# Expert pairs of a routed block: three groups of one-hot sums, and a first weight group of four planes

## The chip, the cores and the metric

The kernel runs on one core of a Trainium2 chip. The metric is the device time of one execution in microseconds (us); lower is better. Everything is float32 at the interface. Engines are named as in the profile: PE (TensorE matmul), PEld (its weight loads), DVE (VectorE), ACT (ScalarE), POOL (GpSimd), SP (SyncE, whose queue issues nearly all DMAs).

## The reference, cut to what matters

The program is a whole block (recurrent branch, sparse attention, routed experts) followed by two layers of a second block. The change touches only the routed experts: 512 tokens, each sent to 2 of 32 experts, each expert a gated pair of products.

```python
def expert_block(args):
    xb, e = args
    hid = jax.nn.silu(xb @ w1[e]) * (xb @ w3[e])     # w1, w3: 1024 x 512
    return hid @ w2[e]                               # w2: 512 x 1024
ys = lax.map(expert_block, (xs, blk_exp)).reshape(n_rows, D_)
out = jax.ops.segment_sum(ys * row_gate[:, None], row_tok, num_segments=T)
...
h = h + g2[:, None, :] * hier_moe(u2, ...)
```

Each expert has three matrices of 2 MiB (2.1 MB), 201 MB in all, and each is read once.

## The kernel before

**The stage.** The experts are worked in 16 pairs (loop at L1452). Each expert has 64 slots, so a pair fills 128 rows: `pair_gather` (L1354) fetches their tokens, `pair_tokens` (L1357) turns them on PE (tile `xgt`) into `xx`. `pair_in` (L1373) makes the two products with W1 and W3 (PE tile `e`, weights `w`), `hidden` (L1269) the gated value on ACT and DVE, `pair_out` (L1400) turns it (`hdt`) and makes the product with W2 (weights `w2r`). These matmuls are float32. `both` (L1368) issues one for each expert of the pair: expert 0 on columns 0 to 63 of the array, expert 1 on columns 64 to 127; each stands in the trace as two instructions. A pair has 64 such instructions on `w` and 32 on `w2r`.

**The one-hot sums.** `outputs` (L1282) scales the result into `y`, splits it into `yh` and `yl` (ACT, then DVE), and returns the generator `combine` (L1295). Each of its 8 steps is one PSUM bank: two matmuls (L1301 with `yl`, L1302 with `yh`) on the whole array, and a DVE add into `h` (L1303). The generator is handed to the `pair_in` after next as `beside`, and in the source one step stands after each of its 8 groups of planes (L1386). PSUM banks for `cmb`, `xgt` and `hdt` come from one tag of three buffers (`tr`).

**Weight buffers.** The 8 planes of W1, and those of W3, are read in four groups of 2 planes, 512 KB per expert and group, in rows of 4 KB, into buffers of the tags PG, PG, WH, WL (L1381). The tag PG has 24 buffers (four are held through this stage: two token pages, `g2R` and a page of small tables), WH and WL have 3 each. W2 is read by `pair_loads` (L1390) as 8 loads of 512 KB into PG. So a pair has 24 loads of 512 KB: 16 PG and 4 each of WH and WL. The tag RAW (3 buffers of 8 KB per partition, 1 MB each) isn't used by the pairs. It serves the dense products before (`TM` and `FM`, L342 and L393) and after.

**The branch.** Ahead of the pairs stands `more(CAP)` (L1449, body L1424 to L1441): a branch that runs only where an expert has more than 64 tokens. Its body, with `expert_in` (L1318) and `expert_out` (L1333), uses RAW, WH and WL. A buffer of a tag that the body uses can't be filled for the pairs ahead of the branch.

**Order.** An engine runs its instructions in one fixed order, but this is not the order of the source: the tile framework chooses it when the program is built, by dependences and its own forecast of when each is ready. The order that came out is read in the trace.

Of the kernel before, what the change touches and what calls it, by code (L numbers as in the profile page):

```python
# [10 lines left out]
F32 = mybir.dt.float32  # L11
F32R = mybir.dt.float32r
# [52 lines left out]
def build(ctx, tc, I, out, dbg=None):  # L65
# [6 lines left out]
    load = nc.sync.dma_start  # L72
# [3 lines left out]
    def t_(shape, dt, tag, name):  # L76
        uid[0] += 1
        return sb.tile(shape, dt, tag=tag, bufs=NB[tag], name=f"{name}_{uid[0]}")

    def pg(name, dt=F32R, shape=(128, 2, 512)):  # L80
        return t_(list(shape), dt, "PG", name)

    def pt_(name, dt=F32R, shape=(128, 2, 512)):
        return t_(list(shape), dt, "PT", name)
# [31 lines left out]
    def sg(name, w=512, dt=F32):  # L116
        return t_([128, w], dt, "SG", name)

    def sa(name, w=512, dt=F32):
        return t_([128, w], dt, "SA", name)  # L120
# [4 lines left out]
    def mmp(name, tag="mm"):  # L125
        uid[0] += 1
        return pp.tile([128, 512], F32, tag=tag, bufs=dict(mm=4, tr=3, po=1)[tag], name=f"{name}_{uid[0]}")

    def trp(name):
        return mmp(name, "tr")  # L130
# [4 lines left out]
    def f(ap):  # L135
        return ap.bitcast(F32)

    def split(hi, lo, src, eng=None):
        S.copy(hi, src)  # L139
        (eng or V).tensor_tensor(lo, src, f(hi), OP.subtract)  # L140
# [144 lines left out]
    def mm3(ps, l, r, start, stop):  # L285

        mmk(ps, [(l, r)], start, stop)

    def mmk(ps, pairs, start, stop):

        for n, (l, r) in enumerate(pairs):
            PE.matmul(ps, l[0], r[1], start=start and n == 0, stop=False)  # L292
            PE.matmul(ps, l[1], r[0], start=False, stop=False)  # L293
        for n, (l, r) in enumerate(pairs):
            PE.matmul(ps, l[0], r[0], start=False, stop=stop and n == len(pairs) - 1)  # L295
# [287 lines left out]
    ps = fm.tile(4352, 72)  # L583
# [6 lines left out]
    ps = trp("wit")  # L590
# [371 lines left out]
    for d in range(8):  # L962
        ps = fmb.tile(128 * d)
# [7 lines left out]
        p = pg("mT")  # L971
        hi, lo = (p[:, n].rearrange("p (c r) -> p r c", r=8) for n in range(2))
# [112 lines left out]
    ps = trp("lgt")  # L1085
# [37 lines left out]
    ps = trp("rank")  # L1123
# [92 lines left out]
    def normalizer(gvec, bvec, dst, paged=True):  # L1216

        gR = row("lng", gvec, True)
        bR = row("lnb", bvec, True)
        pages = []  # L1220

        def norm(i, v, mv, var, later=None):
            r = rsqrt(var, 1, lambda: V.scalar_tensor_tensor(v, v, mv[:, 0:1], gR, OP.subtract, OP.mult))
            for cs in (slice(0, 512), slice(512, 1024)):
                V.scalar_tensor_tensor(v[:, cs], v[:, cs], r, bR[:, cs], OP.mult, OP.add)
                if not paged:
                    load(dst(i)[:, :, cs], v[:, cs])
            if not paged:
                return
            if later is None:  # L1230
                turn(i, v)
            else:
                later.append(lambda: turn(i, v))

        def turn(i, v):
            if not pages:
                pages.extend(pg("xT") for _ in range(8))
            tk = slice(i * 128, (i + 1) * 128)
            for q in range(2):
                b = trp("xt")  # L1240
                for k in range(4):
                    PE.transpose(b[:, k * 128:(k + 1) * 128], v[:, (4 * q + k) * 128:(4 * q + k + 1) * 128], ident)
                for k in range(4):
                    kk, c = 4 * q + k, slice(k * 128, k * 128 + 128)
                    split(pages[kk][:, 0, tk], pages[kk][:, 1, tk], b[:, c])
            load(dst(i), v)

        return norm, pages
# [6 lines left out]
    def rows_of(t):  # L1255
        return lambda i: t[i * 128:(i + 1) * 128, :]
# [12 lines left out]
    def hidden(p1, p3):  # L1269
        hd = sg("hid")  # L1270
        S.activation(hd, p1, AF.Tanh, scale=0.5)
        V.scalar_tensor_tensor(hd, hd, 1.0, p1, OP.add, OP.mult)
        V.scalar_tensor_tensor(hd, hd, 0.5, p3, OP.mult, OP.mult)
        return hd
# [43 lines left out]
    def expert_in(W1, W3, xh, xl):  # L1318
        pss = []
        for W in (W1, W3):  # L1320
            ps = mmp("e1")
            for q in range(4):
                raw = t_([128, 2, 512], F32, "RAW", "w13")
                load(raw, W[q * 256:(q + 1) * 256, :].rearrange("(k p) n -> p k n", p=128))
                hi = t_([128, 2, 512], F32R, "WH", "wh")
                lo = t_([128, 2, 512], F32R, "WL", "wl")
                split(hi, lo, raw)
                mmk(ps, [((xh[:, 2 * q + k], xl[:, 2 * q + k]), (hi[:, k], lo[:, k])) for k in range(2)],
                    q == 0, q == 3)
            pss.append(ps)  # L1330
        return hidden(*pss)

    def expert_out(hd, W2):  # L1333
        b = trp("hdt")
        for k in range(4):
            PE.transpose(b[:, k * 128:(k + 1) * 128], hd[:, k * 128:(k + 1) * 128], ident)
        hp = pt_("hp")
        split(hp[:, 0], hp[:, 1], b)
        py = [mmp("e2") for _ in range(2)]
        for k in range(4):  # L1340
            raw = t_([128, 1024], F32, "RAW", "w2r")
            load(raw, W2[k * 128:(k + 1) * 128, :])
            hi = t_([128, 1024], F32R, "WH", "wh")
            lo = t_([128, 1024], F32R, "WL", "wl")
            split(hi, lo, raw)
            for m in range(2):
                cs = slice(m * 512, m * 512 + 512)
                ks = slice(k * 128, k * 128 + 128)
                mm3(py[m], (hp[:, 0, ks], hp[:, 1, ks]), (hi[:, cs], lo[:, cs]), k == 0, k == 3)
        return py  # L1350


# [15 lines left out]
    def both(ps, lhs, rhs, start, stop):  # L1368
        for h in range(2):
            hs = slice(CAP * h, CAP * h + CAP)  # L1370
            PE.matmul(ps[hs], lhs[:, hs], rhs[h], start=start, stop=stop)  # L1371

    def pair_in(j, xT, beside):  # L1373
        pss = []
        for nm in ("moe_w1", "moe_w3"):
            W = [I[nm][0, 2 * j + h].rearrange("(p a) n -> p a n", a=8) for h in range(2)]
            ps = mmp("e1")
            for q in range(4):
                ws = []
                for h in range(2):  # L1380
                    raw = t_([128, 2, 512], F32, ("PG", "PG", "WH", "WL")[q], "w13")  # L1381
                    load(raw, W[h][:, 2 * q:2 * q + 2])
                    ws.append(raw)
                for k in range(2):
                    both(ps, xT[:, 2 * q + k], [w[:, k] for w in ws], q + k == 0, q + k == 4)
                next(beside, None)  # L1386
            pss.append(ps)
        return hidden(*pss)

    def pair_loads(j):  # L1390
        W = [I["moe_w2"][0, 2 * j + h].rearrange("(p a) n -> p a n", a=4) for h in range(2)]
        ws = []
        for k in range(4):
            for h in range(2):
                raw = pg("w2r", F32, (128, 1024))
                load(raw, W[h][:, k])
                ws.append(raw)
        return ws

    def pair_out(j, hd, ws):  # L1400
        b = trp("hdt")
        cols = hd.rearrange("p (a j) -> p j a", j=4)
        for k in range(4):
            PE.transpose(b[:, k * 128:(k + 1) * 128], cols[:, k], ident)
        hp = sg("hp")
        S.copy(hp, b)
        py = [mmp("e2") for _ in range(2)]
        for k in range(4):
            for m in range(2):
                cs = slice(m * 512, m * 512 + 512)  # L1410
                both(py[m], hp[:, k * 128:k * 128 + 128], [w[:, cs] for w in ws[2 * k:2 * k + 2]], k == 0, k == 3)
        return outputs(py, gt0[:, j:j + 1], rows0[:, :, j])
# [33 lines left out]
    beside = iter(())  # L1446
# [5 lines left out]
    for j in range(17):  # L1452
# [7 lines left out]
        if j == 16:  # L1460
            fgR = row("fgR", I["final_g"])
            norm, xT = normalizer(I["ln_in_g_2"], I["ln_in_b_2"], rows_of(xres[0]))
            nav_tm = nav_weights(0).prepare()
        if prev is not None:
            for _ in beside:
                pass
            beside = pair_out(j - 1, prev, pair_loads(j - 1))
# [477 lines left out]
    xT, nav_tm = layer(0, xT, nav_tm, xres[0], xres[1], rows_of(xres[2]))  # L1945
# [32 lines left out]
```

## Time and profile before

| | us |
|---|---|
| median of 3 runs | 3155.69 (3153.24 to 3157.79) |
| the profiled execution | 3154.16 |
| its span, first to last instruction | 3152.4 |
| PE busy in the span | 2970.1 (94%) |
| DVE, ACT, POOL busy | 1848.6, 1131.5, 279.6 |
| expert stage, from the first expert matmul to the last | 664.5 to 1206 |
| TensorE clock granted, mean | 0.984 |

The span was recorded in one execution of 3154.16 us, 1.5 us under the median. All rows below are of that execution. Times in rows are us from the span's start unless marked ns; a row's "idle before" names what ended the idle time. "PEclk" is the granted share of TensorE's full clock, "DMA" the mean busy share of the core's 16 DMA engines.

### The profile page before, as it was taken

How to read it: one execution, taken by the hardware profiler on the slowest of the kernel's cores; microseconds unless marked ns; L12 is line 12 of the kernel's file. 1: busy time of each engine (PE TensorE's matmuls, PEld its weight loads, DVE VectorE, ACT ScalarE, POOL GpSimd, SP SyncE). 2: the span in 40 equal slices, each digit the busy share in tenths (PEclk: the TensorE clock that was granted, in tenths of full speed). 3: DMA queues.
4: the chain of work that ended last, by engine and by line, in shares of the span. 5: the costliest groups of instructions: out<-in, count | busy, mean ns of one | idle time of the engine just before them, and what ended most of it. 6: DMA issues, size and time to landing. Idle time of an engine off the chain costs nothing.

```text
span 3152.4 us, 36476 instructions
## 1 busy us (share of the span) xinstructions
PE 2970.1 (94%) x13749; PEld 2204.3 (70%) x13749; DVE 1848.6 (59%) x3521; ACT 1131.5 (36%) x1986; POOL 279.6 (9%) x263
## 2 busy tenths in 40 slices
PE   6988999979999998999999999999999999999998
PEld 5766777733333335878867788888888876788887
DVE  6899888633223227555589754434545588764434
ACT  4555244210000003444567332222444576432221
POOL 2133000300000000221000200000221000200000
PEclk9989999989999999999999999999999999999999
DMA  6222756679999995432233623243433234632341
GB/s 222 92 90 65 233 185 195 208 289 353 362 372 377 358 376 193 137 114 94 76 112 111 231 100 107 92 142 100 147 117 101 79 99 116 225 107 93 107 139 62
DMA packets 296257, 534.17 MB, mean 169 GB/s; under 512 B 30279, under 2 KB 172789, under 8 KB 296071
## 3 DMA queue, kind: packets, MB, share of 16 engines
q1 hardware_dynamic: 293480, 527.46, 48.5%
q0 software_dynamic: 2304, 4.20, 0.5%
q8 instruction: 110, 1.80, 0.2%
q14 instruction: 77, 0.62, 0.1%
q10 hardware_dynamic: 286, 0.09, 0.0%
HBM read 486.50 MB, written 44.38 MB: 168 GB/s over the span
## 4 chain that ended last, share of the span: by engine, by line
PE 64%; DVE 7%; issue 3%; DMA 2%; ACT 2%; POOL 1%; SPq 0%; DVEq 0%; POOLq 0%; ACTq 0%
PE e L1371 12%; PE fm L292 9%; PE fm L295 9%; PE fm L293 9%; PE ffo L295 2%; PE ffo L293 2%; PE ffo L292 2%; PE cmb L1301 1%; PE cmb L1302 1%; POOL tl L1634 1%; DVE xT L140 1%; DMA w2r<-in_moe_w_dram 1%; PE mix L292 1%; PE mix L295 1%; PE mix L293 1%
## 5 line engine op out<-in xcount | busy, mean ns | idle before, releaser
L140 DVE TENSOR_TENSOR wl<-raw,wh 128x1024 fp32r<-128x1024 f32 (+3 forms) x403 | 462.3, 1149 | 313.8 <-ACT wh L139 312.2
L139 ACT CAST wh<-raw 128x1024 fp32r<-128x1024 f32 (+3 forms) x403 | 388.6, 966 | 543.0 <-PE fm L295 224.2
L292 PE MATMUL fm<-xT,wh 128*128 128x512 f32 (+1 forms) x1264 | 481.9, 384 | 0.0
L293 PE MATMUL fm<-xT,wl 128*128 128x512 f32 (+1 forms) x1264 | 479.9, 382 | 1.3 <-DVE wl L140 1.3
L295 PE MATMUL fm<-xT,wh 128*128 128x512 f32 (+1 forms) x1264 | 301.9, 381 | 0.0
L1371 PE MATMUL e<-w,xx 128*64 128x512 f32 x1024 | 293.8, 605 | 0.0
L293 PEld LDWEIGHTS fm<-xT,wl 128*128 128x128 f32 x1264 | 238.2, 188 | 46.7 <-DVE wl L140 1.7
L292 PEld LDWEIGHTS fm<-xT,wh 128*128 128x128 f32 x1264 | 238.2, 189 | 45.1
L295 PEld LDWEIGHTS fm<-xT,wh 128*128 128x128 f32 x1264 | 231.6, 188 | 45.5
L1371 PEld LDWEIGHTS e<-w,xx 128*64 128x64 f32 x1024 | 79.2, 137 | 138.6 <-issue 130.0
L293 PE MATMUL fm<-uT,wl 128*128 128x512 f32 (+1 forms) x360 | 145.3, 403 | 3.8 <-DVE wl L140 3.8
L1303 DVE TENSOR_TENSOR h<-h,cmb 128x512 f32<-128x512 f32 x128 | 84.6, 686 | 109.2 <-PE cmb L1302 108.5
L1371 PE MATMUL e<-w2r,hp 128*64 128x512 f32 x512 | 141.9, 607 | 3.6 <-DMA w2r<-in_moe_w_dram 2.1
L292 PE MATMUL fm<-uT,wh 128*128 128x512 f32 (+1 forms) x360 | 145.0, 404 | 0.0
L292 PE MATMUL ffo<-wl,hid 128*128 128x512 f32 x352 | 137.1, 390 | 0.0
L293 PE MATMUL ffo<-wh,hid 128*128 128x512 f32 x352 | 136.9, 389 | 0.0
L1371 PEld LDWEIGHTS e<-w2r,hp 128*64 128x64 f32 x512 | 52.8, 137 | 87.9 <-issue 64.5
L1921 DVE SCALAR_TENSOR_TENSOR ffs<-ffs,fm 128x512 f32<-128x512 f32 x44 | 30.3, 688 | 137.7 <-ACT ffs L1920 137.7
L295 PE MATMUL ffo<-wh,hid 128*128 128x512 f32 x352 | 108.4, 389 | 0.0
L139 ACT CAST yh<-y 128x512 fp32r<-128x512 f32 x32 | 19.8, 618 | 224.2 <-DVE y L1292 224.2
L1923 DVE SCALAR_TENSOR_TENSOR ffs<-ffs,fm 128x512 f32<-128x512 f32 x44 | 30.3, 688 | 114.4 <-PE fm L295 114.4
L1634 POOL TENSOR_TENSOR tl<-ml,tl 128x512 f32<-128x512 f32 x32 | 47.7, 1497 | 554.3 <-DVE tl L1630 540.6
(603 smaller groups left out, 5955.6 us busy)
## 6 DMA issues: line engine op xcount, KB each, us to landing
w<-in_moe_w_dram SPq DMA_DIRECT2D x256, 512.0 KB
raw<-in_w_in_dram SPq DMA_DIRECT2D x71, 1024.0 KB
w2r<-in_moe_w_dram SPq DMA_DIRECT2D x128, 512.0 KB
raw<-in_w_ffn_in_dram SPq DMA_DIRECT2D x44, 1024.0 KB
raw<-in_w_mod_dram SPq DMA_DIRECT2D x42, 512.0 KB
raw<-in_w_ffn_out_dram SPq DMA_DIRECT2D x20, 1024.0 KB
raw<-in_w_out_dram SPq DMA_DIRECT2D x12, 1024.0 KB
t_d<-bg SPq DMA_DIRECT2D x48, 256.0 KB
```

The costliest lines, as they stand in the source:

```text
L139: S.copy(hi, src)
L140: (eng or V).tensor_tensor(lo, src, f(hi), OP.subtract)
L292: PE.matmul(ps, l[0], r[1], start=start and n == 0, stop=False)
L293: PE.matmul(ps, l[1], r[0], start=False, stop=False)
L295: PE.matmul(ps, l[0], r[0], start=False, stop=stop and n == len(pairs) - 1)
L1301: PE.matmul(ps, pl, yl[:, cs], start=True, stop=False)
L1302: PE.matmul(ps, pl, yh[:, cs], start=False, stop=True)
L1303: V.tensor_tensor(h1[i][m], h1[i][m], ps, OP.add)
L1371: PE.matmul(ps[hs], lhs[:, hs], rhs[h], start=start, stop=stop)
L1634: G.tensor_tensor(th, m, th, OP.add)
L1921: V.scalar_tensor_tensor(s, s, 1.0, pgt, OP.add, OP.mult)
L1923: V.scalar_tensor_tensor(s, s, 0.5, pup, OP.mult, OP.mult)
```

## The change

Three edits, all in the routed experts.

1. `pair_in`: W1 is read in groups of 4, 2 and 2 planes (tags RAW, PG, PG), W3 in four groups of 2 (PG, PG, WH, WL). The group of 4 planes is 1 MB per expert in rows of 8 KB. A pair then has 22 loads: 2 RAW of 1 MB, 16 PG, 2 WH and 2 WL of 512 KB.
2. `pair_in`: the steps of `combine` stand in the source in three groups: 3 after the second group of W1, 3 after the first group of W3, 2 after the third of W3.
3. `expert_in` and `expert_out`, in the branch's body only: the raw weights go to buffers of 512 columns of the tags SG and SA instead of RAW.

```diff
@@ expert_in @@
             for q in range(4):
-                raw = t_([128, 2, 512], F32, "RAW", "w13")
-                load(raw, W[q * 256:(q + 1) * 256, :].rearrange("(k p) n -> p k n", p=128))
                 hi = t_([128, 2, 512], F32R, "WH", "wh")
                 lo = t_([128, 2, 512], F32R, "WL", "wl")
-                split(hi, lo, raw)
+                for k in range(2):
+                    raw = sg("w13")
+                    load(raw, W[(2 * q + k) * 128:(2 * q + k + 1) * 128, :])
+                    split(hi[:, k], lo[:, k], raw)
@@ expert_out @@
         for k in range(4):
-            raw = t_([128, 1024], F32, "RAW", "w2r")
-            load(raw, W2[k * 128:(k + 1) * 128, :])
...
             for m in range(2):
...
+                raw = sa("w2r")
+                load(raw, W2[ks, m * 512:m * 512 + 512])
+                split(hi[:, m], lo[:, m], raw)
+                mm3(py[m], (hp[:, 0, ks], hp[:, 1, ks]), (hi[:, m], lo[:, m]), k == 0, k == 3)
@@ pair_in @@
-        for nm in ("moe_w1", "moe_w3"):
+        for n, nm in enumerate(("moe_w1", "moe_w3")):
             W = [I[nm][0, 2 * j + h].rearrange("(p a) n -> p a n", a=8) for h in range(2)]
             ps = mmp("e1")
-            for q in range(4):
+            k = 0
+            for tag, w, banks in ((("RAW", 4, 0), ("PG", 2, 3), ("PG", 2, 0)), (("PG", 2, 3), ("PG", 2, 0), ("WH", 2, 2), ("WL", 2, 0)))[n]:
                 ws = []
                 for h in range(2):
-                    raw = t_([128, 2, 512], F32, ("PG", "PG", "WH", "WL")[q], "w13")
-                    load(raw, W[h][:, 2 * q:2 * q + 2])
+                    raw = t_([128, w, 512], F32, tag, "w13")
+                    load(raw, W[h][:, k:k + w])
                     ws.append(raw)
-                for k in range(2):
-                    both(ps, xT[:, 2 * q + k], [w[:, k] for w in ws], q + k == 0, q + k == 4)
-                next(beside, None)
+                for m in range(w):
+                    both(ps, xT[:, k + m], [r[:, m] for r in ws], k + m == 0, k + m == 7)
+                k += w
+                for _ in range(banks):
+                    next(beside, None)
             pss.append(ps)
```

## Rows read from the trace of the kernel before

**Rows 1.** The page's 40 equal slices: PE and DMA, busy tenths.
```profile
PE   6988999979999998999999999999999999999998
DMA  6222756679999995432233623243433234632341
```

**Rows 2.** Windows: stretch, then busy us (count) by engine, PEclk, DMA share, GB/s.
```profile
645.00:650.00 5.00, 0.01 (x1) 0.01 (x1) 4.74 (x27) 0.43 (x3) 0.00 (x0) 0.68 0.00 0
...
655.00:660.00 5.00, 1.91 (x9) 1.77 (x9) 1.97 (x13) 0.00 (x0) 1.95 (x2) 0.50 0.22 49
...
662.70:1196.00 533.30, 514.70 (x1938) 193.70 (x1938) 165.57 (x246) 48.95 (x81) 14.07 (x14) 1.00 0.96 367
...
770.79:1152.19 381.40, 370.45 (x1366) 138.06 (x1364) 116.20 (x173) 32.62 (x56) 8.93 (x9) 1.00 0.96 369
```

**Rows 3.** The same view: one pair, a stretch at full DMA share, and a later dense stage.
```profile
910.71:945.07 34.36, 33.35 (x126) 12.47 (x124) 10.79 (x16) 2.97 (x6) 0.99 (x1) 1.00 0.95 369
...
1150.00:1200.00 50.00, 45.24 (x157) 16.59 (x156) 20.74 (x29) 6.96 (x10) 0.00 (x0) 0.97 1.00 383
...
2000.00:2060.00 60.00, 60.00 (x267) 49.67 (x266) 26.41 (x34) 14.17 (x18) 0.00 (x0) 1.00 0.32 105
```

**Rows 4.** Chain that ended last, pair 1 and pair 2: start us, us, engine, tile, line, count.
```profile
720.67 1.87 PE e L1371 x8
722.54 0.43 PE cmb L1301
722.97 0.23 PE cmb L1302
...
735.12 0.74 DVE y L1292
```

**Rows 5.** The same chain in one later pair, and its first row of the last whole period.
```profile
913.40 1.86 PE e L1371 x6
915.26 0.43 PE cmb L1302
915.69 0.24 PE cmb L1301
915.92 0.23 PE cmb L1302
916.15 1.00 PE e L1371 x2
...
929.62 15.43 PE e L1371 x64
...
1152.19 0.75 DVE y L1292
```

**Rows 6.** Timeline of PE: start, us, line, operation, tile, shape, count [idle before <- releaser].
```profile
662.66 1.94 PE L1364 MATMUL xgt<-ident,xg 128*128 128x128 f32 x8 [5.76 <-DVEq L1424]
...
912.12 0.50 PE L1301 MATMUL cmb<-yl,place 128*128 128x512 f32 x1 [0.96 <-DVE yl L140]
...
1187.26 0.50 PE L1301 MATMUL cmb<-yl,place 128*128 128x512 f32 x1 [1.44 <-DVE yl L140]
...
1191.67 0.40 PE L1302 MATMUL cmb<-yh,place 128*128 128x512 f32 x1
```

**Rows 7.** What the SP queue waited for, 735 to 1152 us: total, times, longest.
```profile
SPq L1382 <- PE e L1371: 132.2, 24, 8.7
SPq L1382 <- DMA w2r<-in_moe_w_dram: 94.0, 96, 1.6
```

**Rows 8.** Timeline of SP around the branch: DMA issues in order, with counts.
```profile
588.61 21.55 SPq L1382 DMA_DIRECT2D w<-in_moe_w_dram  x11
...
637.69 0.44 SPq L1396 DMA_DIRECT2D w2r<-in_moe_w_dram  x1
662.73 2.85 SPq L1382 DMA_DIRECT2D w<-in_moe_w_dram  x6
```

**Rows 9.** Groups by line, 735.12 to 1152.19 us: busy, mean ns | idle before, releasers.
```profile
L1303 DVE TENSOR_TENSOR h<-h,cmb 128x512 f32<-128x512 f32 x96 | 63.9, 686 | 90.6 <-PE cmb L1302 90.1
```

More of the change, by code (lines that the diff above doesn't have):

```diff
@@ L1340, in expert_out @@
         for k in range(4):
-            raw = t_([128, 1024], F32, "RAW", "w2r")
-            load(raw, W2[k * 128:(k + 1) * 128, :])
-            hi = t_([128, 1024], F32R, "WH", "wh")
-            lo = t_([128, 1024], F32R, "WL", "wl")
-            split(hi, lo, raw)
+            ks = slice(k * 128, k * 128 + 128)
+            hi = t_([128, 2, 512], F32R, "WH", "wh")
+            lo = t_([128, 2, 512], F32R, "WL", "wl")
             for m in range(2):
-                cs = slice(m * 512, m * 512 + 512)
-                ks = slice(k * 128, k * 128 + 128)
-                mm3(py[m], (hp[:, 0, ks], hp[:, 1, ks]), (hi[:, cs], lo[:, cs]), k == 0, k == 3)
+                raw = sa("w2r")
+                load(raw, W2[ks, m * 512:m * 512 + 512])
+                split(hi[:, m], lo[:, m], raw)
+                mm3(py[m], (hp[:, 0, ks], hp[:, 1, ks]), (hi[:, m], lo[:, m]), k == 0, k == 3)
         return py
```

## The prediction

> **What bounds the kernel now.** I read the slices of the page first, to see where the change can act [rows 1]: from about 660 to 1206 us, and nowhere else, PE and DMA are both at 9 tenths. So two limits lie close together, and the question is which one holds the other. The windows give the size [rows 2]: from 662.70 to 1196.00 the stage moves 533.3 us x 367 GB/s = 195.7 MB at a DMA share of 0.96, while PE is busy 514.70 of 533.30. In the eleven periods from 770.79 to 1152.19 a pair takes 381.40 / 11 = 34.67 us, and moves 34.67 x 369 = 12.8 MB.
>
> Three views tell the limits apart. In one pair PE is idle 1.0 of 34.36 us [rows 3], and nearly all of that is one wait of 0.96 us for `yl` [rows 6]: weights are there when PE wants them. The SP queue, on the other side, spent 132.2 us of twelve periods waiting for PE to free a weight buffer, 24 times [rows 7]: two a period, as many as W3's loads that find WH and WL still full. It waited for earlier DMAs as well (94.0 us in one row), so the reserve is small: the share of 0.96 becomes 1.00 where PE does not hold the loads back, and the rate there is 383 GB/s [rows 3]. I read: PE's order is the bound, transport stands 4% behind it.
>
> Where PE's 34.67 us go is in the chain. In pair 1, eight matmuls of `e` in one run take 1.87 us, and one bank of sums 0.43 + 0.23 [rows 4]; this is the order of the source. From pair 2 on the order is another: 2 matmuls, three of the sums, 6 matmuls, three of the sums [rows 5]. Two on their own take 1.00 and six take 1.86, so these eight need 2.86 instead of 1.87. The two are those of expert 0 alone; the other half of the array stands empty for them, and expert 1's are missing their partner later. The split lies where expert 0's load is there and expert 1's isn't yet, in the forecast that ordered them. Four groups of a pair (all of W1) are split so, until no sums and turns are left to put in; after that 64 run in 15.43 us [rows 5], 0.24 each. In pair 1 a group with its bank took 1.87 + 0.43 + 0.23 = 2.53 us, less than a split group alone. The first of the twelve periods starts at 735.12 [rows 4] and the last ends at 1152.19 [rows 5].
>
> **The change part by part.** *Split groups.* Each costs 2.86 - 1.87 = 0.99 us, four a pair: 3.96 of the 34.67 [rows 4, 5]. The first group is now two loads of 1 MB. The gap between expert 0's and expert 1's data there is twice as long, so it takes twice as many of the 28 instructions that are put in (16 sums, 12 turns), and the remaining fourteen matmuls of the group run whole. I take two split groups instead of four: -1.98 a pair. Ends: one left (-2.97), or all four (0).
>
> *Runs of sums.* The sums of a pair stand in six runs now; the first matmul of a run takes 0.43 against 0.23 or 0.24 of the next [rows 5]. Three runs instead of six save 3 x 0.20 = 0.60; ends 0 and -0.80. The Trainium skill, page "TensorEngine Tiling (Array Packing)", section "Tiling Modes", says that changing the tiling mode drains TensorE. By that rule alone, fewer switches would be the whole of this edit: 12 x 0.60 = 7 us. The trace agrees that a switch costs, but shows 0.20 us for it, and 0.99 for a split group beside it.
>
> *What grouping adds.* If the sums come straight behind the W2 product, PE waits for the whole chain `y`, `yh`, `yl`: 1.44 us, as at 1187.26, instead of 0.96 [rows 6]: +0.48, ends 0 and +0.48. Queued behind that wait is all of `e`, PE being in order. And a bank must be added into `h` before the fourth next one has a buffer: DVE needs 686 ns a bank [rows 9], PE 0.47. Eight banks in a row took from 1187.26 to 1192.07 [rows 6], 4.81 us against 16 x 0.234 = 3.74. In runs of three or four banks I take a third of that difference, +0.36; ends 0 and +1.07. DVE has the room: 63.9 us of adds in 417.
>
> PE's period: 34.67 - 1.98 - 0.60 + 0.48 + 0.36 = 32.9 us; ends 30.9 and 36.2.
>
> *Buffers.* W1 and W3 used four WH and four WL loads a pair with three buffers each; now it is two and two, and two of RAW with three buffers. The two SP waits a period for W3's buffers should go, since the next use of a WH buffer is a pair later. What is late next is transport itself: 12.8 MB at 383 GB/s is 33.4 us. This lies above PE's 32.9, so the bound passes to the DMAs.
>
> *Ahead of the branch.* SP issued 20 loads of experts from 588.61 to 637.69, as many as PG has free buffers, and then six at once at 662.73, three WH and three WL, behind the branch [rows 8]. In between the DMAs stood still: share 0.00 at 645 to 650 [rows 2]. With RAW out of the branch's body three loads of 1 MB can go ahead of it: 3.15 MB less to move behind 662.7. SP must wait for the dense product of the mix to release RAW, and the stores of `u_d` stand behind it; the idle stretch covers several us of that, and without this cover the delay would reach the token gather. I put it at 0.
>
> *Rows of 8 KB.* A sixth of the bytes. No row shows such a load. The nearest are the full rate of 383 with 4 KB rows and, with 1 KB rows, 105 GB/s at a share of 0.32, or 328 [rows 3]: 17% in two doublings. One doubling for a sixth of the bytes is at most 1.4%, 7 us, in either direction. I take 0, the value of the nearest row.
>
> *The branch's body.* No instruction of L1425 to L1441 ran, so its new loads cost nothing. PE waits 5.76 us behind the branch [rows 6]; a body of another length could move that by a us, up or down; I take 0. If a count passed 64 the body would run, and 8 loads of W2 in place of 4 would show.
>
> *The sum.* 195.7 - 3.15 = 192.6 MB. At full share, 383 GB/s, that is 502.8 us, 30.5 less than 533.3. At today's 367 it is 524.7, 8.6 less. I take a share of 0.98 (375 GB/s), halfway between the two rows, because limits of 32.9 and 33.4 us still delay each other: 513.5 us, 19.8 less. What comes behind 1196 (the last W2 product and its sums) is unchanged. 3154.2 - 19.8 = 3134 us, made against the profiled execution, which lies 1.5 us under the median.
>
> **The rivals.** *Transport is full already.* Share 0.96 may be all there is with gaps between loads, and the 132 us of SP waits only order what would wait anyway. For it: SP's waits for DMAs are as long together. Against it: 383 at share 1.00. It gives 0 to 8.6 us, the lead alone: 3150. The Trainium skill, page "DMA: Bandwidth & Descriptors", section "Bandwidth", names about 358 GB/s as what HBM gives one core; by that rule no order of PE could bring anything. The 367 over 533 us is already above it, so the trace does not agree with it as a ceiling.
>
> *It does not do what it says.* The order comes from the build's forecast, not from the source: today "eight single banks" are six runs. All four groups may stay split. Then PE gains 0.60 and pays 0 to 0.84 a pair: 3151, give or take 6. For it: the pattern of rows 5 has stood in twelve pairs alike.
>
> *Slower.* The sums land as one block ahead of `e`, and the splits stay. The place is the head of each pair: PE waits 0.48 longer and the banks cost 1.07 by DVE's pace; fewer runs may not come. 36.2 - 34.67 = 1.5 us, twelve times: +18, 3172. It decides as soon as these costs exceed what fewer splits give, that is if fewer than two of four splits go. Against it: with longer gaps between loads that wait is PE's idle time anyway.
>
> *More than forecast.* One split or none, full share, and 8 KB rows that bring their 7 us: 30 to 37 less, 3117 to 3124.
>
> **How the numbers follow.** Forecast 0.54 (3124 to 3144), more 0.12, transport full 0.12, not what it says 0.12, slower 0.10. A measurement of this kernel can tell about 0.2%, 6.3 us. A quarter of the two middle rivals passes it by the lead, so faster 0.72, within 0.2% 0.18, slower 0.10. The range that leaves out the slower case and the lowest corner is 3117 to 3156.
>
> **What would show it.** Split groups: runs of 14 or 16 of `e` near a pair's start, and fewer 1.00-us pairs; if four of them stay, that step is wrong. Runs: first sums at 0.43, two to four times a pair. Bound: DMA share 0.98 or more, PE idle for `w` or `w2r`, SP's waits for PE under 40 us; a share of 0.96 with SP waits of the same size would say that PE still binds. Lead: three loads of 1 MB ahead of 650 us. Period: 33 to 34 us. The forecast falls if PE waits for `yl` or for DVE's adds by over 2 us a pair, or if the DMA rate at full share drops under 375.

## The result and the profile after

| | before | after |
|---|---|---|
| median, us (4 runs each, side by side) | 3154.61 | 3115.91 (3112.92 to 3118.41) |
| ratio, 95% interval | | 0.9876, 0.9858 to 0.9893 |
| the profiled execution's span, us | 3152.4 | 3113.7 |

The changed kernel is 38.7 us faster; 19.8 were forecast, and 3115.9 lies 1 us below the range. Pairs are numbered 0 to 15 here, as in the prediction's "pair 1". The times at which VectorE began `y` (the end of a pair's W2 product) divide the 38.7 us of span:

| stretch | before | after | difference |
|---|---|---|---|
| span's start to the first `xgt` of the stage | 662.66 | 659.50 | -3.2 |
| to `y` of pair 0 | 42.20 | 40.20 | -2.0 |
| pairs 1 and 2 | 65.07 | 56.47 | -8.6 |
| pairs 3 to 13, eleven periods | 381.40 | 359.84 | -21.6 |
| pairs 14 and 15 | 53.53 | 47.43 | -6.1 |
| from there to the end | 1947.5 | 1950.2 | +2.7 |

A period of pairs 3 to 13 fell from 34.67 to 32.71 us: most of them are 32.47, two are 33.7 and 33.8. The first row belongs to no edit that I can name: over all kernels below, the first `xgt` stands anywhere from 659.5 to 664.1 us, and order_before and head_sums, whose loads up to there are alike, differ by 2.9 us.

The windows of after (stretch, busy us and count for PE, PEld, DVE, ACT and POOL, PEclk, DMA share, GB/s); they answer to [rows 2, 3]:

```profile
790.71:1116.82 326.11, 309.77 (x1240) 114.88 (x1240) 103.14 (x157) 29.30 (x50) 7.93 (x8) 0.99 1.02 403
790.71:823.18 32.47, 30.85 (x124) 11.38 (x124) 10.54 (x17) 2.94 (x5) 0.99 (x1) 1.00 1.02 411
```

One pair moves bytes at 411 GB/s with a DMA share of 1.02. The rate of 383 at a share of 1.00 in [rows 3], on which my ceiling for transport rested, was no ceiling: a share can read above 1.

The chain that ended last in after, one pair (start us, us, engine, tile, line, count); it answers to [rows 5]:

```profile
790.71 0.75 DVE y L1292
...
792.23 0.47 PE cmb L1301
...
793.46 1.00 PE e L1371 x2
794.46 0.43 PE cmb L1302
...
797.00 5.29 PE e L1371 x22
802.29 0.43 PE cmb L1301
802.72 1.00 PE e L1371 x2
803.72 0.43 PE cmb L1302
...
804.74 1.86 PE e L1371 x6
806.60 0.76 PE xgt L1364 x5
807.35 1.00 PE e L1371 x2
...
809.26 13.89 PE e L1371 x62
...
823.18 0.75 DVE y L1292
```

Three groups are still split (three rows `e` x2 at 1.00 us), and the sums stand in four runs, the first of them at the pair's head, right behind `yl`. The last run of `e` takes 13.89 us for 62, where [rows 5] has 15.43 for 64; the one run of 64 in after, at the end of pair 14, has 13.98. The timeline of PE in before (start, us, line, operation, tile, shape, count) shows where its 15.43 us went, and where the first of its four splits stood:

```profile
910.12 1.04 PE L1371 MATMUL e<-w,xx 128*64 128x512 f32 x2
...
929.55 7.09 PE L1371 MATMUL e<-w,xx 128*64 128x512 f32 x32
936.47 8.57 PE L1371 MATMUL e<-w2r,hp 128*64 128x512 f32 x32
```

The product with W3 takes 7.09 us for 32 instructions, the one with W2 8.57. PEld, which loads the array, waited for `w2r` until 940.54, 941.82 and 943.10 us, steps of 1.28 us: W2's loads came a little late, one after the other, and TensorE shows no idle time there because its instructions then started one by one (942.30, 942.73, 943.10) where they had started in twos (938.18, 938.24). From 770 to 1070 us PEld's waits for `w2r` fell from 7.1 us in before to 4.0 in after, 30 times to 14. And the first split of before (910.12) stood ahead of the sums, beside the wait for `yl`; in after all three stand behind it.

What TensorE waited for by far the most from 770 to 1070 us of after (total, times, longest), and what SP waited for from 727 to 1116 us; the second answers to [rows 7]:

```profile
PE cmb L1301 <- DVE yl L140: 14.3, 9, 1.8
```

```profile
SPq L1384 <- DMA w<-in_moe_w_dram: 84.8, 61, 2.8
...
SPq L1384 <- PE e L1371: 52.6, 19, 8.0
```

So TensorE stands 1.6 us a pair for `yl` (8.6 us in nine pairs of before, now 14.3) and is never idle for weights, while SP still waits for TensorE 19 times. No DMA stands in the chain of the pair above. TensorE's order binds after the change as before it, but transport is now close behind: a DMA share of 1.02 where it was 0.96.

SP around the branch in after, answering to [rows 8]:

```profile
588.78 20.65 SPq L1384 DMA_DIRECT2D w<-in_moe_w_dram  x14
...
627.44 1.75 SPq L1384 DMA_DIRECT2D w<-in_moe_w_dram  x3
629.28 1.60 SPq L1400 DMA_DIRECT2D w2r<-in_moe_w_dram  x3
...
659.56 6.58 SPq L1384 DMA_DIRECT2D w<-in_moe_w_dram  x7
```

23 loads go ahead of the branch, three of them of 1 MB, where 20 of 512 KB went before.

### The profile page after: what moved, and what is told of

It reads as the page before. It is cut to its first block, busy times and chain, and to the rows that moved or that the text cites. A ratio compares the mean times of both kernels' runs of the same rounds, so it can differ in the third digit from the quotient of the medians.

```text
span 3113.7 us, 36560 instructions
## 1 busy us (share of the span) xinstructions
PE 2926.9 (94%) x13749; PEld 2189.3 (70%) x13749; DVE 1842.7 (59%) x3521; ACT 1131.0 (36%) x1986; POOL 280.7 (9%) x263
## 4 chain that ended last, share of the span: by engine, by line
PE 64%; DVE 6%; issue 3%; DMA 2%; ACT 2%; POOL 1%; SPq 0%; DVEq 0%; POOLq 0%; ACTq 0%
PE e L1371 11%; PE fm L292 9%; PE fm L293 9%; PE fm L295 9%; PE ffo L295 3%; PE ffo L292 3%; PE ffo L293 3%; PE cmb L1301 1%; PE cmb L1302 1%; POOL tl L1638 1%; PE mix L292 1%; PE mix L293 1%; PE mix L295 1%; PE xgt L1364 1%; DMA w<-in_moe_w_dram 1%
## 5 line engine op out<-in xcount | busy, mean ns | idle before, releaser
L1371 PE MATMUL e<-w,xx 128*64 128x512 f32 x1024 | 269.0, 601 | 0.0
L1371 PE MATMUL e<-w2r,hp 128*64 128x512 f32 x512 | 122.2, 593 | 2.7 <-ACT hp L1410 2.7
L1924 ACT ACTIVATE ffs<-fm 128x512 f32<-128x512 f32 x44 | 26.3, 598 | 188.7 <-PE fm L295 188.7
L1371 PEld LDWEIGHTS e<-w2r,hp 128*64 128x64 f32 x512 | 40.4, 137 | 73.3 <-issue 63.4
```

## The experiments

All twelve, each beside runs of the kernel before on the same chip (medians of before 3155.2, 3156.0 and 3155.6). "Period" is the mean of pairs 3 to 13 by the starts of `y`; share, rate and SP's waits for TensorE are those of 770 to 1070 us.

| label | us | ratio to before, 95% | period | DMA share, GB/s | SP's longest row for PE `e`, us |
|---|---|---|---|---|---|
| before | 3155 | | 34.67 | 0.96, 367 | 98.3 |
| after | 3115.9 | 0.9858 to 0.9893 | 32.71 | 1.02, 405 | 32.6 |
| sums_only | 3156.7 | 0.9995 to 1.0014 | 34.65 | 0.96, 367 | 98.3 |
| loads_only | 3120.6 | 0.9867 to 0.9900 | 32.95 | 1.01, 399 | 101.9 |
| rows_4k | 3111.1 | 0.9842 to 0.9874 | 32.11 | 1.03, 408 | 1.4 |
| order_rows_4k | 3102.6 | 0.9808 to 0.9851 | 31.04 | 1.03, 408 | 2.1 |
| light_before | 3113.9, one run | | 31.70 | 1.02, 401 | 53.7 |
| light_after | 3096.3, one run | | 31.33 | 1.02, 410 | 2.5 |
| old_body | 3129.5 | 0.9895 to 0.9929 | 32.83 | 1.02, 405 | 69.1 |
| order_lead | 3093.9 | 0.9778 to 0.9821 | 30.90 | 1.02, 410 | 6.5 |
| order_before | 3111.6 | 0.9842 to 0.9874 | 31.43 | 1.03, 408 | 35.2 |
| order_after | 3097.4 | 0.9798 to 0.9839 | 30.91 | 1.02, 410 | 6.4 |
| split_w3 | 3131.0 | 0.9893 to 0.9937 | 32.77 | 1.01, 392 | 61.2 |
| head_sums | 3129.8 | 0.9895 to 0.9942 | 32.54 | 1.01, 396 | 67.6 |

### The grouping of the sums

sums_only is the kernel before with the sums in three groups and the loads as they were; loads_only is the kernel after with the sums spread again.

```diff
-                next(beside, None)
+                for _ in range(((0, 3, 0, 0), (3, 0, 2, 0))[n][q]):
+                    next(beside, None)
```

> The kernel before with only the sums regrouped in the source (3, 3 and 2 banks behind the second group of W1, the first and the third of W3); loads and buffers as before. Built, PE's order differs from that of before in pair 1 alone; from pair 2 on it is the same split order. Theory (buffers and the order that follows from the loads carry the gain): 0 to 3 us faster than before, 3152 to 3155, period 34.7 us. Rival (the grouping of the sums carries it): about 3116, period 32.5.

```diff
-((("RAW", 4, 0), ("PG", 2, 3), ("PG", 2, 0)), (("PG", 2, 3), ("PG", 2, 0), ("WH", 2, 2), ("WL", 2, 0)))[n]
+((("RAW", 4, 2), ("PG", 2, 1), ("PG", 2, 1)), (("PG", 2, 1), ("PG", 2, 1), ("WH", 2, 1), ("WL", 2, 1)))[n]
```

> The changed kernel with the sums spread again in the source (2 banks behind the group of four planes, then one behind each group). PE's order from pair 3 on is that of the changed kernel. Theory (loads and buffers): within 3 us of the changed kernel, 3114 to 3119, period 32.5. Rival (grouping): about 3150, near the kernel before.

Grouping alone changes nothing: 3156.7 against 3155.2, and the same period, share and waits as before. With the new loads and the old spreading the time is 3120.6, 1.6 us above the range of its theory, its interval overlapping that of after. The chain of sums_only (columns as above) shows why grouping alone does nothing:

```profile
913.57 0.50 PE cmb L1301
914.06 1.86 PE e L1371 x6
915.92 0.43 PE cmb L1302
...
916.82 1.00 PE e L1371 x2
```

It is the order of [rows 5] again: 6 of `e`, three of the sums, 2 of `e`. The place of the sums in the source hardly reaches TensorE's order; the gain comes with the loads. That the build decides it by when it expects their data is my reading of this, and not shown. In loads_only SP waits for TensorE three times as long as in after (101.9 us against 32.6), at a period only 0.24 us longer: the length of these waits alone does not set the time.

### The length of the rows

rows_4k fills each buffer of four planes by two loads of 512 KB; order_rows_4k does the same in the kernel order_after (below).

```diff
-                    load(raw, W[h][:, k:k + w])
+                    for o in range(0, w, 2):
+                        load(raw[:, o:o + 2], W[h][:, k + o:k + o + 2])
```

> The changed kernel, but each 1 MB buffer is filled by two loads of 512 KB with rows of 4 KB: the same buffers, 24 loads a pair, no 8 KB rows. Theory (the rate does not hang on the rows): 3110 to 3122, 395 to 411 GB/s in the steady pairs. Rival (8 KB rows raise the rate, 4 KB rows stop at 383 GB/s): period 33.4 us, 3125 to 3135.

> The changed kernel with the pair's matmuls in source order on TensorE, and each weight buffer of four chunks filled by two loads of 4 KB rows in the place of one of 8 KB rows. In source order the DMAs are what the pairs wait for (31.4 us a pair, 410 GB/s), so the rows' length has nowhere to hide. Theory, the length of the rows carries nothing: 3094 to 3100 us, 31 to 32 us a pair, 405 to 411 GB/s. Rival, longer rows move faster and TensorE hid it in the run with 4 KB rows and the other order: 3 to 5% on 31.4 us over 11 pairs, so 3108 us or more at 390 to 398 GB/s.

Without any row of 8 KB the changed kernel takes 3111.1, 4.8 us less than with them. TensorE's order is another in that run, so this isn't yet the rows' price. One line from its timeline of PE, then the chain of the same pair:

```profile
889.41 1.02 PE L1371 MATMUL e<-w,xx 128*64 128x512 f32 x2
```

```profile
894.74 3.58 PE e L1371 x14
898.32 0.43 PE cmb L1301
...
898.98 1.00 PE e L1371 x2
...
900.88 1.86 PE e L1371 x6
...
903.50 1.00 PE e L1371 x2
...
907.80 13.98 PE e L1371 x64
```

Three groups are split here too, but the halves of the first (889.41) stand ahead of the sums, beside the wait for `yl`, so that two rows of 1.00 us are left in the chain instead of three; the period is 0.6 us shorter. With the order held fixed (order_after against order_rows_4k) shorter rows cost 5.2 us by the medians, with overlapping intervals, and 408 against 410 GB/s. That is 2.6 us above the upper end of the first theory and 5.4 below the lower end of its rival: by the medians 8 KB rows are worth some 0.5%, which these runs do not tell from noise, and they do not carry the gain.

### What transport takes

light_before and light_after cut every `e` matmul of the pairs but the first of each sum to 32 columns: most of the expert products is left out. The loads and their buffers are as they were; TensorE's order, which the build chose anew, is another, with split groups in it too.

```diff
+            n = 512 if start else 32
-            PE.matmul(ps[hs], lhs[:, hs], rhs[h], start=start, stop=stop)
+            PE.matmul(ps[hs, 0:n], lhs[:, hs], rhs[h][:, 0:n], start=start, stop=stop)
```

> The kernel before with the pairs' matmuls cut to 32 columns, but for the first of each accumulation, so that most of the expert products is left out; all loads, buffers and sums stay. It shows what transport does alone with 4 KB rows. Theory (transport had room before): over 400 GB/s in the steady pairs, period 31 to 32 us, total 3095 to 3115. Rival (383 GB/s is what 4 KB rows give): period 33.4 us or more, total 3130 or more.

> The changed kernel with the pairs' matmuls cut to 32 columns, but for the first of each accumulation, so that most of the expert products is left out. Transport alone with a sixth of the bytes in 8 KB rows. Theory (rows do not matter): the same rate as the kernel before cut in the same way, within 2%, period 31 to 32 us. Rival (8 KB rows matter): 5% or more above it.

The window of light_before, 770 to 1070 us, columns as above:

```profile
770.00:1070.00 300.00, 211.22 (x1195) 127.44 (x1193) 98.55 (x152) 27.59 (x48) 8.90 (x9) 0.75 1.02 401
```

With TensorE busy 211 of 300 us, though at a mean granted clock of 0.75, the old loads run at 401 GB/s and 31.70 us a pair, the new ones at 410 and 31.33 (2.2% more, just outside the 2% of the theory). TensorE is idle for weights in light_before, 56.0 us for `w` and 32.5 for `w2r`. SP still waits 53.7 us for TensorE, so what the old loads can do may lie a little higher yet. So the old form of the loads allowed nearly the rate that after reaches, 31.3 to 31.7 us a pair against the 33.4 of the prediction, and before stood 3 us a pair above it.

### The lead ahead of the branch

old_body is after with the branch's body as before (it uses RAW again, so no RAW load passes the branch). order_lead is order_after with WH and WL out of the body, too.

```diff
             for q in range(4):
+                raw = t_([128, 2, 512], F32, "RAW", "w13")
+                load(raw, W[q * 256:(q + 1) * 256, :].rearrange("(k p) n -> p k n", p=128))
...
-                    raw = sg("w13")
```

> The changed kernel with the branch's body as before, which uses RAW: no load into RAW can go ahead of the branch. Built, pair 2 has the split order instead of the source's. Theory (the lead of 3 MB and the whole pair 2 are worth 5 to 8 us): 3120 to 3125. Rival (the lead is hidden anyway, PE binds): 3114 to 3118.

```diff
-                hi = t_([128, 2, 512], F32R, "WH", "wh")
-                lo = t_([128, 2, 512], F32R, "WL", "wl")
                 for k in range(2):
                     raw = sg("w13")
...
+                    hi, lo = sa("wh", 512, F32R), sa("wl", 512, F32R)
```

> The changed kernel in source order, with the branch's body splitting its weights in the small buffers instead of the two large ones that the pair's weights use too, so that 3 MB more of expert weights may start ahead of the branch. Theory, the pairs wait for the DMAs, so what is in ahead of the branch comes off the end: 3 MB at 400 GB/s is 7.5 us at most, less what the body's own loads and the run-up to the branch take from it: 3088 to 3093 us, and the first chunk of the first pair no later. Rival, the lead is already as long as the idle DMA time ahead of the branch, or the body gets slower by its smaller buffers: 3095 to 3102 us.

Without the lead the time is 3129.5, 13.6 more than after and 4.5 above the range of its theory. In the two traces 3.8 of these lie ahead of the first `xgt` (the scatter named above), 4.4 between there and `y` of pair 0, and 6.0 in pairs 1 and 2. Pair 2 then has the split order, where after runs it in the order of the source:

```profile
739.66 0.42 PE cmb L1301
740.08 1.90 PE e L1371 x2
...
745.01 5.29 PE e L1371 x22
750.30 0.43 PE cmb L1301
750.73 1.00 PE e L1371 x2
```

So the lead is worth about 10 us, and the part in pairs 1 and 2 comes by TensorE's order. Still more lead shows no such gain: order_lead is 3.5 us under order_after by the medians, with overlapping intervals, and between its two expected ranges. The two traces differ by 0.5 us in span: 2.6 gained ahead of the first `xgt` (660.76 against 663.31) and 0.7 in pair 0, and most of it given back behind. I count the further lead as hidden.

### TensorE's order, held to that of the source

order_before and order_after are the two kernels with nothing changed but that the matmuls of `both` and of the sums keep their program order.

```diff
-            PE.matmul(ps[hs], lhs[:, hs], rhs[h], start=start, stop=stop)
+            tc.keep_in_program_order(PE.matmul(ps[hs], lhs[:, hs], rhs[h], start=start, stop=stop))
...
-                    PE.matmul(ps, pl, yl[:, cs], start=True, stop=False)
+                    tc.keep_in_program_order(PE.matmul(ps, pl, yl[:, cs], start=True, stop=False))
```

> The kernel before with the pairs' matmuls and sums pinned to the order of the source on PE: no split groups; loads and buffers unchanged. If PE's split order alone was the bound, the period falls to 31.5 to 32.5 us and the time to 3110 to 3125. If the three WH and WL buffers hold the loads back, SP goes on waiting for PE and the period stays above 33.5: 3138 to 3155.

> The changed kernel with the pairs' matmuls and sums pinned to the order of the source on PE: no group is split but one in W3, sums in three runs, none of them first in a pair. PE's period by rows is 28 to 29 us. Theory (transport ends at about 411 GB/s, 31.5 to 32 us a pair): 3104 to 3111. Rival (PE's order still binds, or waiting for loads in order costs what it saves): 3114 or more.

This is the decisive pair. With the old loads, the old buffers, the old body and the sums in single banks, order alone takes the kernel before to 3111.6, 44 us less, at least as far as the whole change took it. SP issues the pairs' loads in the same order in both, so that isn't what differs. In the timeline of PE (start, us, line, operation, tile, shape, count) two of its eight unsplit groups, and then two rows of its chain:

```profile
865.07 1.96 PE L1371 MATMUL e<-w,xx 128*64 128x512 f32 x8
866.96 0.50 PE L1301 MATMUL cmb<-yl,place 128*128 128x512 f32 x1
867.30 0.40 PE L1302 MATMUL cmb<-yh,place 128*128 128x512 f32 x1
867.62 1.98 PE L1371 MATMUL e<-w,xx 128*64 128x512 f32 x8
```

```profile
866.36 10.21 DMA w<-in_moe_w_dram
...
876.59 10.22 DMA w2r<-in_moe_w_dram
```

A group with its bank takes 867.62 - 865.07 = 2.55 us, close to the 2.53 of [rows 4] for pair 1 of before. From 770 to 1070 us the chain of order_before goes from DMA to DMA, with next to nothing in between; SP still waits for TensorE there, 35.2 us, but 1.9 at the longest (7.3 in before). In order_after, 6.6 us below the range of its first theory, TensorE itself is idle for weights, as the prediction had it of the kernel after:

```profile
PE e L1371 <- DMA w<-in_moe_w_dram: 9.1, 9, 1.7
```

That is from 756 to 1100 us; the rate is 410 GB/s. In these two kernels, and neither in before nor in after, the bound has passed to the DMAs.

### Splits and the head of the pair, each alone

Both start from order_before. split_w3 puts a bank of sums between the two halves of a matmul of W3, four times a pair; head_sums puts all eight banks ahead of the pair's first weight, with no split.

```diff
+            if h == 0:
+                between()
...
+                         (lambda: next(beside, None)) if nm == "moe_w3" and k == 0 else (lambda: None))
```

> The kernel before with its pair in source order, but four pairs of the third weight's column-half matmuls pulled apart: a bank of one-hot sums stands between the two halves, four times in a pair. Theory, a split costs TensorE what the trace of before shows for two halves alone (1.00 us in the place of about 0.44) and some switches more: four splits add 2 to 4 us to a pair that takes 31.4 us in source order, so 33.5 to 35 us a pair over 11 pairs and more, 3135 to 3155 us. Rival, the splits are harmless and what held the kernel before was the wait of the first bank for yl and W2 loads just in time: 31 to 32 us a pair and 3108 to 3118 us, as in source order without splits.

```diff
+            for _ in beside if nm == "moe_w1" else ():
+                pass
...
-                next(beside, None)
```

> The kernel before in source order, with all eight banks of one-hot sums right behind the W2 products of the pair ahead, ahead of this pair's first weight; no split, one run of sums, and TensorE stands for yl and then goes at VectorE's pace of 0.69 us a bank. Theory, what the sums cost TensorE at the head is the wait of 1.5 us and 0.2 us a bank, less than the splits: 30.5 to 32 us a pair, close to what the DMAs allow (31.4), 3110 to 3125 us. Rival, it was the wait at the head and VectorE's pace that held the kernel before: 34 to 35 us a pair, 3140 to 3155 us.

split_w3 took 3131.0, 19.4 us more than order_before, every period 32.77. That is below the first theory's figures (33.5 to 35) and well above the rival's (3108 to 3118): splits cost, but I had added them to 31.4, and 31.4 is transport's, not TensorE's. The timeline of PE shows the price itself:

```profile
850.04 1.93 PE L1371 MATMUL e<-w,xx 128*64 128x512 f32 x6
851.90 0.50 PE L1301 MATMUL cmb<-yl,place 128*128 128x512 f32 x1
...
852.56 1.07 PE L1371 MATMUL e<-w,xx 128*64 128x512 f32 x2
```

From 850.04 to the bank is 1.86 us, and the two halves alone hold the array 1.00 (the next bank begins at 853.56): 2.86 for eight against 1.89 in order_before. So a split costs 0.97 us of TensorE's time; by these, four make up to 3.9 a pair. Over order_before's period only 1.34 shows; the rest falls into time for which the DMAs bind in order_before.

The same run says that splits are not all that held before. split_w3 has four of them, with the loads and buffers of before, and still takes 24.6 us less than before. Its W2 product is not late, and no sum waits for `yl`:

```profile
863.21 7.09 PE L1371 MATMUL e<-w2r,hp 128*64 128x512 f32 x32 [0.68 <-ACT hp L1410]
```

So the old buffers don't make W2's loads late by themselves; with the order of before they do, 8.57 us against 7.09 a pair.

head_sums was 3129.8 us, and a period 32.54 in the profiled execution, the fastest of its four (3122.8): above the first theory (30.5 to 32), below the rival (34 to 35). The longest of PE's waits, 770 to 1070 us:

```profile
PE cmb L1301 <- DVE yl L140: 13.8, 9, 1.5
```

The wait for `yl` is 1.5 us a pair, as expected. With no split at all it is slower than order_before by 18 us, so a block of sums at the head is nearly as dear as four splits. How much of that is the wait, how much VectorE's pace and how much the late W2 loads that come with it, this run doesn't tell apart.

## Why the prediction was wrong

*What bounds the kernel now: right in the main.* TensorE's order was the bound; order_before shows it with nothing else edited. "Weights are there when PE wants them" was not right: W2's came late, some 1.5 us a pair, which showed as slower `e` and not as idle time. "Transport stands 4% behind it" was too little: it stood at 31.3 to 31.7 us a pair (light_before, light_after), 9 to 10% behind.

*Term (transport): the step that failed.* I took 383 GB/s, the rate at share 1.00 in [rows 3], for the ceiling, and 375 for the forecast; 12.8 MB in 33.4 us "lies above PE's 32.9, so the bound passes to the DMAs". Measured: 403 over pairs 4 to 13 of after, 411 in one pair, 408 to 410 over 300 us in the kernels of fixed order. The row that I took as nearest came from a stretch that reaches into the next stage, and the share is no fraction that ends at 1. The trace of before could have told me, had I asked for the fastest stretch instead of one at share 1.00: from 720 to 740 us it moves 405 GB/s at a share of 1.02. The Trainium skill, page "HBM Reference", section "Specifications (TRN2)", says that a core streaming alone measures well above its share of 358 GB/s, about 425. The runs agree with it as far as they go, with 411 at most; by the same sentence the 358 that the prediction cited is what each of two cores gets when both stream.

*TensorE's period: nearly right, and with it the sum would have been near.* 32.9 was worked out, 32.71 measured. By parts it was not as good; the errors cancel, and that is luck:

| term, us a pair | predicted | after, by the chain rows |
|---|---|---|
| split groups | -1.98 (four to two) | -0.99 (four to three) |
| runs of sums | -0.60 (six to three) | -0.40 (six to four) |
| wait for `yl` | +0.48 | +0.6 |
| VectorE's pace | +0.36 | +0.25 (two rows of sums at 0.35 and 0.36 in place of 0.23) |
| run with W3 and W2 | none | -1.45 (15.43 to 13.98 for 64) |
| sum | -1.74 | -2.0 |

The measured column goes by rows of one pair of each, the last term by the run of 64 at the end of pair 14; its sum lies near the difference of the two pairs, 34.36 - 32.47 = 1.89. The rows on splits and on `yl` belong together: no split stands beside the wait any more, and the wait is longer without it. So about 0.5 of the 2 us is TensorE's order by itself, and the rest is the term that wasn't there. [Rows 5] showed 64 in 15.43 us, "0.24 each", beside eight in 1.87, 0.23 each; I took the difference for the price of the tile, and it was lateness of W2's loads. The prediction's "four a pair" at 0.99 us also counts the split beside the wait at its full price. With the transport term struck out, the prediction's own numbers give 11 x 1.77 = 19.5 us for the eleven periods, where 21.6 came.

*The lead: right in size.* 8.4 us in the sum (3.15 MB at 375 GB/s), about 10 by old_body. But it was counted as bytes that needn't be moved; it came as an earlier pair 0 and as pairs 1 and 2 in a better order.

*The end of the stage: missed.* "What comes behind 1196 is unchanged" left out that the last W2 loads of before ended the chain (two rows of 9.11 and 11.46 us of `w2r` from 1172 to 1196). In after they are no longer late, and pairs 14 and 15 take 6.1 us less.

*Rows of 8 KB: right at 0*; some 0.5%, not clear of noise. The estimate that led there took the 105 GB/s of [rows 3] for loads with rows of 1 KB, but half of the bytes of that stretch came in packets of 2 KB. *The branch's body: right at 0 for its instructions.* TensorE's wait behind the branch is 5.89 us, against 5.76 [rows 6].

*"It does not do what it says" was half right.* The grouping of the sums, which names the change, did not reach TensorE's order (sums_only); the other half of the change carried the gain. I had given that case 0.12 and a time of 3151, because I tied the splits to both.

*The signs I named:* three 1.00-us pairs in place of four, runs of 22 and not of 14 or 16, a share of 1.02, three loads of 1 MB ahead of 650 us. SP's waits for TensorE were 52.6 us and not under 40, and TensorE had no idle time for `w` or `w2r`: two of the three signs of transport are missing, and TensorE still binds. Only the share spoke for transport. SP's waits were a poor sign besides: loads_only has 101.9 us of them from 770 to 1070 us at nearly the period of after.

What stays open: the 3.2 us ahead of the stage, the 2.7 given back behind it, and the shares inside head_sums. Open, too, is how much of after's 21.6 us in the eleven periods the new buffers gave and how much the new order, since no run holds the order of before with the buffers of after.

## What to carry to other kernels

A mean rate over its busy share is no ceiling; read the fastest stretch of the same transfers before a bound is said to pass to them, or take the other engine's work away and look. Where the build orders an engine by its forecast, the order is a lever of its own: matmuls that fill half the array each should stand together with their partner, and holding them and the sums in program order was worth 44 us here, at least as much as the whole change. On top of the change it gave 3097.4 us, and 3093.9 with the smaller body, both faster than either kernel. Idle time alone does not show late weights: where two halves of the array work side by side, compare runs of the same product as well (8.57 us against 7.09).

## What the runs showed of the hardware

The DMA share of the profile read 1.01 to 1.03 in stretches of 300 us at 392 to 410 GB/s. At a share of 1.02 the rate was 401 (light_before), 405 (after) or 410 (order_after), so the share doesn't rank full stretches. In the kernels before and after, two matmuls on 64 columns that stand alone between matmuls of the whole array took 1.00 us, half of what eight in a row took (1.87), and the first whole-array matmul behind them 0.43 in place of 0.23.
